# A two-layer decoder trunk on one core: the last group of the first layer's down product done with seven products, folded into the next layer by quarters

## The chip, the cores and the metric

The kernel runs on 1 core of a Trainium2 chip. The metric is the device time of one execution in microseconds (us). The engines are PE (TensorE matmul, with PEld its weight loads), DVE (VectorE), ACT (ScalarE), POOL (GpSimd) and SP (SyncE, which issues DMAs here). TensorE's granted clock is at its upper level, 2.4 GHz, through the whole execution of the kernel before (mean 0.998 of it).

## The reference, cut to what matters

```python
def reference(x, ...):                                # x: 512 tokens x 1024, float32
    for layer in range(2):
        h = rms_norm(x, g_mix[layer])
        x = x + mixer(h, ...)                         # layer 0: dilated + windowed attention; layer 1: forgetting attention
        h = rms_norm(x, g_mlp[layer])
        x = x + squared_relu_mlp(h, w_up[layer], w_down[layer])
    return x

def squared_relu_mlp(h, w_up, w_down):                # 1024 -> 4096 -> 1024
    u = jnp.einsum("bsd,df->bsf", h, w_up)
    return jnp.einsum("bsf,fd->bsd", jnp.square(jax.nn.relu(u)), w_down)
```

## The kernel before, in words

Everything is float32. A float32 product is done as three matmuls of a rounded type: each operand is split into a high part (`whi`, `hn[:, 0]`, a cast) and a low part (`wlo`, `hn[:, 1]`, operand minus high part), and hi·hi, lo·hi and hi·lo are added up in PSUM. So each weight tile passes ACT (or POOL), which casts, and DVE (or POOL), which subtracts, before PE uses it. There are 7 buffers for high and 7 for low parts.

**The MLP** (function `mlp`) is a list of `items`, run position by position; PE's work is written out in that order, and the weights of a position are prepared 6 positions ahead (`prep(n + R)`). Item `("U", u)` makes 256 of the 4096 hidden features for all 512 tokens (4 positions of 12 matmuls, 128x512). After four U items their part of the down product follows, as item `("T", g)`: a seven-product scheme for 2x2 blocks. Hidden features and tokens are halved, the output is a 2x2 grid of quarters `rest[e, t]` (512 output columns e, 256 tokens t), and seven products of sums of blocks take the place of eight. Each has 4 positions of 6 matmuls, so a T item has 28 positions and 168 matmuls, and 2 more that open the banks of `Y`. `ORDER` gives the products' order and their PSUM banks X, Y, Z; when one is done, `combine_t` adds it into a quarter on DVE, scaled by the token's 1/rms² (`r2col`). `sums_t` makes the sums of weight blocks on DVE, `t_sums` those of the hidden features.

**The end of layer 0 before.** Groups 0 to 2 are T items. The last group is done directly, as four items `("E", g, dp)`: for each pair of 128 output features, 4 positions of 12 matmuls into `dn`, output features on the partitions and tokens along the row. That is the form in which layer 1 needs its input, so `direct_end` adds `dn` to the residual (`back`), makes `hn` (hi and lo, 128x512, one tile for each of 8 chunks of features), squares it into `ssum2`, and sends it to memory (`xsp`). The quarters of groups 0 to 2 have tokens on the partitions: `fold(c)` transposes them on PE during the U items before, into `rT`, and adds them to `back`. The hidden features of the last group are scaled by 1/rms² with DVE (`part`), which needs 1/rms² along the row: a matmul with `ones` (`r2`) and reciprocals.

**The start of layer 1.** `layer_attention` projects first `v` of four heads and the forget logits (`vf_c`, 96 matmuls of 128x272 into four banks `pj0` to `pj3`, one for 128 tokens each, over the 8 chunks `hn`). After `STATS` steps of 12 matmuls it calls `stats`: `token_sums` sums squares over features (`pc`), and DVE makes 1/rms from them (`col_stats`, 13 small operations, into `rcol`). `rcol` scales the forget logits (`fz`, transposed on PE into `pz`) and `v`; then the banks `pj` are free for the next projection, of q and k (`qk_c(0)`), whose first matmul stands behind `pz` on PE. `PAT_START` and `PAT_FIRST` name the engines that cast and subtract for `vf_c`.

The last group of layer 1 is a T item already. The scheduler orders each engine's instructions; those pinned (`pin`) keep the written order.

Of the kernel before, what the change touches and what calls it, by code (L numbers as in the profile page):

```python
# [35 lines left out]
PAT_START = (('act', 'dve'), ('act', 'dve'))  # L36
WARM = 30
# [32 lines left out]
def trunk(ctx, tc, x, b_sinks, w_out_even, b_forget, w_out_odd, w_up, w_down, xt, gains, w_in_even, w_in_odd, out):  # L70
# [127 lines left out]
    def layer_attention(li, hT, w_in, w_out, stats=None):  # L198


        with ExitStack() as c2:
# [370 lines left out]
            else:  # L572
# [191 lines left out]
    def mlp(li, accs, attention_end, last):  # L764
# [7 lines left out]
        with ExitStack() as c2:  # L772
# [76 lines left out]
            def load(j):  # L849
# [52 lines left out]
            ORDER = ((11, "b11", "X"), (1, "t1", "Z"), (2, "t2", "Y"), (4, "b22", "Z"), (3, "t3", "Y"), (12, "b21", "X"),  # L902
# [41 lines left out]

            def direct(j, p, hi, lo):

                if p % 2 == 0:
                    res[j, p] = bank(("pA", "pB")[items[j][2] % 2], "dn")
                o = res[j, p - p % 2]
                for k in range(4):  # L950
                    v = store[12 + k, p % 2]
                    mm3(o, hi[:, k], lo[:, k], v[:, 0], v[:, 1], p % 2 == 0 and k == 0, bool(p % 2 and k == 3), k == 0)

            def direct_end(j, p):

                if p % 2 == 0:
                    return
                dp = items[j][2]
                c = 2 * dp + p // 2
                a = back[dp][:, p // 2]  # L960
                if c == 0:
                    res["ssum2"] = consts.tile([P, 512], F32, tag="ssum", name="ssum2")
                vec(nc.vector.tensor_add(a, res[j, p - 1], a))
                h = slot("hn")
                g = gcol[:, 8 * (li + 1) + c:8 * (li + 1) + c + 1]
                sca(nc.scalar.activation(h[:, 0], a, AF.Copy, scale=g))
                vec(nc.vector.scalar_tensor_tensor(h[:, 1], a, g, h[:, 0].bitcast(F32), op0=OP.mult, op1=OP.subtract))
                squares(c, a, res["ssum2"], sq_pool)
                hn.append(h)
                if c % 2:  # L970
                    nc.scalar.dma_start(xsp[dp], back[dp])
# [40 lines left out]
            def combine_t(j, p):  # L1012
# [4 lines left out]
                for b in range(2):  # L1017
# [12 lines left out]
                    if j == len(items) - 1 and i in (4, 3, 12, 22):  # L1030
# [11 lines left out]
            def come_back(dp):  # L1042
                a = mp.tile([P, 2, 512], F32, tag="mraw", bufs=4, name="back")
# [3 lines left out]
            def fold(c):  # L1047

                pt = bank("pB", "rT")
                for m in range(NT):  # L1050
                    pin("p", nc.tensor.transpose(pt[:, m * P:(m + 1) * P],
                                                 rest[c // 4, m // 2][:, m % 2, c % 4 * P:(c % 4 + 1) * P], ident))
                a = back[c // 2][:, c % 2]
                vec(nc.vector.tensor_add(a, pt, a))
# [14 lines left out]
            def unit_end(j):  # L1069
# [8 lines left out]
                def whole(e):  # L1078
                    s = slot("s") if u < 15 else mp.tile([P, 2, 512], F32R, tag="t24", bufs=2, name="s")
                    halves(s[:, 0], s[:, 1], v[:, e])  # L1080
                    store[u, e] = s

                def part(e):

                    sca(nc.scalar.activation(v[:, e], v[:, e], AF.Square))
                    vec(nc.vector.tensor_mul(v[:, e], v[:, e], ssum))
                    whole(e)
                    if u == 15:
                        catch_up()

                if not last and u >= 12:
                    return [lambda: part(0), lambda: part(1)]

# [12 lines left out]
                def t_part(i):  # L1106
                    if i and u % 4 == 0 and u:
# [16 lines left out]
            def plan(j):  # L1124
# [5 lines left out]
                if not last and u >= 12:  # L1130
                    offs = FIN12 if u == 12 else (0, 1)
                else:
                    offs = FIN15 if u == 15 else FIND if u % 4 == 0 and u else FIN
# [14 lines left out]
            else:  # L1148
                for dp in range(4):
                    at(LEAVE[dp], lambda dp=dp: leave(dp))  # L1150
                    at(first[16] + BACK[dp], lambda dp=dp: come_back(dp))
                for c in range(DC):
                    at(first[17] + FOLD[c], lambda c=c: fold(c))
                for n in range(8):
                    at(first[6] + n, lambda n=n: vec(nc.vector.reciprocal(ssum[:, n * 64:n * 64 + 64],
                                                                         ssum[:, n * 64:n * 64 + 64])))

            def end(n):
# [3 lines left out]
                {"U": up_end, "E": direct_end, "T": combine_t}[items[j][0]](j, p)  # L1162
                if not last and items[j] == ("U", 15):
                    if p % 2:
                        unit_end(j)[p // 2]()
                elif n + 1 == NP or pos[n + 1][0] != j:
                    plan(j)
# [15 lines left out]
            for n, (j, p) in enumerate(pos):  # L1183
# [3 lines left out]
                {"U": up, "E": direct, "T": product_t}[items[j][0]](j, p, hi, lo)  # L1187
# [58 lines left out]
```

## Time and profile before

| | before |
|---|---|
| time, median of 3 (lowest to highest) | 1157.34 us (1156.99 to 1157.52) |
| profiled execution: its own time | 1157.34 us |
| profiled execution: span of its instructions | 1155.2 us |
| PE busy, share of the span | 1140.4 us, 99% |
| DVE busy | 862.1 us, 75% |
| ACT busy | 649.2 us, 56% |
| POOL busy | 197.5 us, 17% |
| last group of layer 0, first to last matmul `dn` | 519.85 to 563.14 us |

The span is what the profiler saw of the program's instructions; 2.1 us of the time lie around it. A matmul's duration in the rows is its way through the array; matmuls overlap, and what one costs is the distance between two starts.

### The profile page before, as it was taken

What the parts mean: (1) busy time and instruction counts of PE and PEld (TensorE: products, weight loads), DVE (VectorE), ACT (ScalarE), POOL (GpSimd) and SP (SyncE); (2) the same over time, 40 slices, a digit from 0 to 9 for tenths busy, and PEclk for the clock granted to TensorE, in tenths of its full rate; (3) what the DMA queues carried; (4) which work ended last, traced back from release to release, by engine and by line L of the source; (5) the groups of instructions that cost most, each with busy time, mean ns of one, the idle gap of its engine ahead of it and who ended that gap; (6) DMA issues with size and microseconds to landing.
All of it is one profiled execution on the core that took longest, in us unless ns stands there. A gap on an engine that the chain in (4) does not pass through costs nothing.

```text
span 1155.2 us, 16365 instructions
## 1 busy us (share of the span) xinstructions
PE 1140.4 (99%) x5758; PEld 956.8 (83%) x5758; DVE 862.1 (75%) x1791; ACT 649.2 (56%) x1344; POOL 197.5 (17%) x292
## 2 busy tenths in 40 slices
PE   9999999999999999999999999999999999999998
PEld 7987887888888888888988888888888888888887
DVE  7878999967857858755647877878848759669586
ACT  7555867656656455444326675665656455465452
POOL 0445524100000000000345545432000000000000
PEclk9999999999999999999999999999999999999999
DMA  8432114530531630723543333344420722523403
GB/s 289 132 92 74 40 54 146 200 129 37 185 107 37 219 110 4 250 72 105 154 123 108 103 106 99 106 128 128 164 74 25 231 73 70 186 73 115 150 28 110
DMA packets 91329, 133.83 MB, mean 116 GB/s; under 512 B 6112, under 2 KB 54240, under 8 KB 91248
## 3 DMA queue, kind: packets, MB, share of 16 engines
q1 hardware_dynamic: 90208, 130.63, 35.5%
q10 hardware_dynamic: 1040, 2.16, 0.5%
q8 instruction: 45, 0.74, 0.3%
q14 instruction: 36, 0.29, 0.1%
HBM read 119.63 MB, written 6.32 MB: 109 GB/s over the span
## 4 chain that ended last, share of the span: by engine, by line
PE 86%; DVE 6%; DMA 2%; ACT 2%; issue 2%; POOL 1%; SPq 0%; DVEq 0%; POOLq 0%; ACTq 0%
PE up L166 10%; PE up L170 10%; PE up L169 10%; PE pj L235 4%; PE pj L237 4%; PE pj L236 4%; PE Y L999 3%; PE Y L998 3%; PE Y L996 3%; PE O L406 3%; PE PT L386 2%; PE Z L999 2%; PE X L998 2%; PE Z L998 2%; PE X L999 2%; PE X L996 2%
## 5 line engine op out<-in xcount | busy, mean ns | idle before, releaser
L166 PE MATMUL up<-xin,whi 128*128 128x512 f32 x512 | 200.8, 392 | 0.0
L794 ACT CAST whi<-wraw 128x512 fp32r<-128x512 f32 x228 | 139.3, 620 | 107.5 <-PE up L170 47.8
L170 PE MATMUL up<-xin,whi 128*128 128x512 f32 x512 | 199.4, 389 | 0.0
L169 PE MATMUL up<-xin,wlo 128*128 128x512 f32 x512 | 199.2, 389 | 0.0
L795 DVE TENSOR_TENSOR wlo<-wraw,whi 128x512 fp32r<-128x512 f32 x228 | 150.6, 686 | 61.2 <-ACT whi L794 60.6
L154 POOL TENSOR_SCALAR whi<-wraw 128x512 fp32r<-128x512 f32 x88 | 58.2, 663 | 462.3 <-PE pj L237 419.8
L170 PEld LDWEIGHTS up<-xin,whi 128*128 128x128 f32 x512 | 96.1, 188 | 20.1
L169 PEld LDWEIGHTS up<-xin,wlo 128*128 128x128 f32 x512 | 96.2, 188 | 19.8 <-issue 0.2
L166 PEld LDWEIGHTS up<-xin,whi 128*128 128x128 f32 x512 | 96.1, 188 | 19.8 <-issue 0.2
L794 ACT CAST whi<-mraw 128x512 fp32r<-128x512 f32 x112 | 68.0, 620 | 53.1 <-DVE mraw L894 22.5
L366 ACT ACTIVATE P<-P,negm 128x128 f32<-128x128 f32 (+5 forms) x128 | 69.4, 543 | 41.9 <-DVE negm L363 39.4
L943 ACT ACTIVATE u<-up 128x512 f32<-128x512 f32 x64 | 38.3, 599 | 91.8 <-PE up L170 91.8
L235 PE MATMUL pj<-whi,hn 128*128 128x512 f32 (+2 forms) x256 | 88.7, 346 | 0.0
L237 PE MATMUL pj<-whi,hn 128*128 128x512 f32 (+2 forms) x256 | 86.9, 339 | 0.0
L236 PE MATMUL pj<-wlo,hn 128*128 128x512 f32 (+2 forms) x256 | 86.8, 339 | 0.0
L795 DVE TENSOR_TENSOR wlo<-mraw,whi 128x512 fp32r<-128x512 f32 x112 | 74.5, 683 | 6.5 <-ACT whi L794 6.4
L815 DVE TENSOR_TENSOR t<-u 128x256 f32<-128x256 f32 x56 | 23.2, 423 | 68.1 <-ACT u L1076 66.2
L157 POOL TENSOR_TENSOR wlo<-wraw,whi 128x512 fp32r<-128x512 f32 x48 | 64.3, 1341 | 21.2 <-ACT whi L152 18.7
L996 PE MATMUL Y<-whi,t 128*128 128x512 f32 x168 | 65.4, 389 | 0.0
L998 PE MATMUL Y<-wlo,t 128*128 128x512 f32 x168 | 65.4, 389 | 0.0
L999 PE MATMUL Y<-whi,t 128*128 128x512 f32 x168 | 65.4, 389 | 0.0
L374 POOL TENSOR_SCALAR P<-P,rden 128x256 f32<-128x256 f32 (+2 forms) x96 | 48.5, 508 | 83.2 <-DVE rden L369 77.7
(213 smaller groups left out, 2788.4 us busy)
## 6 DMA issues: line engine op xcount, KB each, us to landing
wraw<-in_w_up SPq DMA_DIRECT2D x64, 512.0 KB, 4.5
wraw<-in_w_down SPq DMA_DIRECT2D x50, 512.0 KB, 4.1
mraw<-in_w_down SPq DMA_DIRECT2D x28, 512.0 KB, 4.8
wraw<-in_w_in_odd SPq DMA_DIRECT2D x22, 512.0 KB, 3.6
wraw<-in_w_in_even SPq DMA_DIRECT2D x17, 512.0 KB, 4.9
K<-K SPq DMA_DIRECT2D x26, 256.0 KB, 2.9
bias<-csp SPq DMA_DIRECT2D x16, 256.0 KB, 3.3
wraw<-in_w_out_odd SPq DMA_DIRECT2D x8, 512.0 KB, 3.6
```

Of the source, the lines that this page charges most:

```text
L166: m = nc.tensor.matmul(o, wh, xh, start=start, stop=False, skip_group_check=more)
L169: nc.tensor.matmul(o, wl, xh, start=False, stop=False, skip_group_check=more)
L170: nc.tensor.matmul(o, wh, xl, start=False, stop=stop, skip_group_check=more)
L235: nc.tensor.matmul(o, xh, hi[:, :n], start=k == 0, stop=False)
L236: nc.tensor.matmul(o, xh, lo[:, :n], start=False, stop=False)
L237: nc.tensor.matmul(o, xl, hi[:, :n], start=False, stop=k == DC - 1)
L366: nc.scalar.activation(p[:, :ne], p[:, :ne], AF.Exp, scale=-1.0, bias=negm[:, i:i + 1], accum_out=den[:, i:i + 1])
L794: sca(nc.scalar.copy(dst_h, src))
L795: late.append(lambda: vec(nc.vector.tensor_sub(dst_l, src, dst_h.bitcast(F32))))
L996: m = nc.tensor.matmul(o, sh, hi, start=new and k == 0, stop=False, skip_group_check=not new)
L998: nc.tensor.matmul(o, sh, lo, start=False, stop=False, skip_group_check=not new)
L999: nc.tensor.matmul(o, sl, hi, start=False, stop=k == 3, skip_group_check=not new)
```

## The change

The last group of layer 0 becomes a T item like the others. So the E items, `direct`, `direct_end`, the matmul `r2`, its reciprocals and `part` go. All quarters are now complete only in the last group, so `fold` moves there: for each quarter (e, t), when its last product is combined, two half-folds follow, each of 4 transposes, an addition of 128x512, and then, for two chunks of features and 256 tokens, the cast into `hn`, the subtraction, and the squares. `ORDER` puts b21 (X) ahead of t3 (Y) and b22 (Z) in all groups, of both layers, so the quarters become complete in the order (0,0), (1,1), (0,1), (1,0), after positions 15, 19, 23 and 27 of the group. The sums of squares of two halves of features stay apart, so `token_sums` has 8 matmuls in place of 4. `STATS` goes from 3 to 4 and `vf_c`'s low parts move from DVE to POOL.

```diff
+PAT_FIRST = (('act', 'pool'),)
-BACK = (0, 0, 1, 1)
-FOLD = (0, 0, 1, 1, 2, 2, 3, 3)
-STATS = 3
+BACK = (2, 2, 7, 7)
+FOLD = {(0, 0): 17, (1, 1): 21, (0, 1): 25, (1, 0): 28}
+STATS = 4
...
-                    return project([(512, 768), (3072, 3088)], use, PAT_START)
+                    return project([(512, 768), (3072, 3088)], use, PAT_FIRST)
...
-                if last:
-                    return
-                pr = bank("pB", "r2")
-                tc.keep_in_program_order(nc.tensor.matmul(pr, ones, ssum, start=True, stop=True))
...
-                if g < 3 or last:
-                    items.append(("T", g))
-                else:
-                    items += [("E", g, dp) for dp in range(4)]
+                items.append(("T", g))
...
-            LOADS = {-2: 11, -1: 21, 0: 22, 6: 12, 16: 220}
+            LOADS = {-2: 11, -1: 21, 0: 22, 2: 12, 16: 220}
...
-            ORDER = ((11, "b11", "X"), (1, "t1", "Z"), (2, "t2", "Y"), (4, "b22", "Z"), (3, "t3", "Y"), (12, "b21", "X"),
+            ORDER = ((11, "b11", "X"), (1, "t1", "Z"), (2, "t2", "Y"), (12, "b21", "X"), (3, "t3", "Y"), (4, "b22", "Z"),
                      (22, "t4", "Y"))
...
+            def fold(e, t, half):
+                dp = 2 * e + half
...
+                pt = bank("pB", "rT")
+                for cc in range(2):
+                    for b in range(2):
+                        pin("p", nc.tensor.transpose(pt[:, cc * 256 + b * P:cc * 256 + (b + 1) * P],
+                                                     rest[e, t][:, b, (2 * half + cc) * P:(2 * half + cc + 1) * P], ident))
+                ts = slice(t * 256, t * 256 + 256)
+                a = back[dp][:, :, ts]
+                vec(nc.vector.tensor_add(a, pt.rearrange("p (c t) -> p c t", c=2), a))
+                for cc in range(2):
...
+                    sca(nc.scalar.activation(h[:, 0, ts], a[:, cc], AF.Copy, scale=g))
+                    vec(nc.vector.scalar_tensor_tensor(h[:, 1, ts], a[:, cc], g, h[:, 0, ts].bitcast(F32),
+                                                       op0=OP.mult, op1=OP.subtract))
+                ss = res["ss"][:, :, ts]
...
+                    sca(nc.scalar.activation(sq, a, AF.Square))
+                    if (e, t) == (1, 0):
+                        vec(nc.vector.tensor_add(ss, ss, sq))
+                    else:
+                        pool(nc.gpsimd.tensor_add(ss, ss, sq))
...
+                for (e, t), n in FOLD.items():
+                    for half in range(2):
+                        at(first[-1] + n + half, lambda e=e, t=t, half=half: fold(e, t, half))
...
-            return hn, lambda: col_stats(token_sums(res["ssum2"]))
+            return hn, lambda: col_stats(token_sums([res["ss"][:, k] for k in range(2)]))
```

**DVE, in the last group of layer 0, behind the product b21 (X).** `rest_3304` is quarter (0,0) and `rest_3307` quarter (1,1); `wlo` are low parts of the group's own weights; line numbers here are those of the changed file. After the change the instructions stand so:

```order
L990 SCALAR_TENSOR_TENSOR rest_3304<-X_5419,r2col_2798,rest_3304 128x512 [waits PE_49]
L990 SCALAR_TENSOR_TENSOR rest_3304<-X_5420,r2col_2798,rest_3304 128x512 [waits PE_49]
L797 TENSOR_TENSOR wlo_5629<-mraw_5233,whi_5628 128x512 [waits Activation_49]
L797 TENSOR_TENSOR wlo_5641<-mraw_5235,whi_5640 128x512 [waits Activation_49]
L1026 TENSOR_TENSOR back_5470<-rT_5656,back_5470 128x2x256 [waits DMAHW4_49,PE_49]
L1031 SCALAR_TENSOR_TENSOR hn_5653<-back_5470,gcol_81,hn_5653 128x256 [waits Activation_49]
L1031 SCALAR_TENSOR_TENSOR hn_5654<-back_5470,gcol_81,hn_5654 128x256 [waits Activation_49]
L797 TENSOR_TENSOR wlo_5651<-mraw_5235,whi_5650 128x512
L1026 TENSOR_TENSOR back_5472<-rT_5679,back_5472 128x2x256 [waits DMAHW5_49,PE_49]
L1031 SCALAR_TENSOR_TENSOR hn_5677<-back_5472,gcol_81,hn_5677 128x256 [waits Activation_49]
L1031 SCALAR_TENSOR_TENSOR hn_5678<-back_5472,gcol_81,hn_5678 128x256 [waits Activation_49]
L797 TENSOR_TENSOR wlo_5675<-wraw_5539,whi_5674 128x512 [waits DMAHW7_49]
```

Behind these stand the two combines of quarter (1,1). Before, nothing but weights and combines stood between two products of a T item on DVE; the fold is new there, and its subtractions wait for ACT.

**PE, in the same group, at position 22.** `rT_5726` is the first half-fold of quarter (1,1), `pj0` the first matmul of layer 1's `vf_c`, which the scheduler has put between two positions of Z. The rows are those of the change:

```order
L960 MATMUL Z_5488<-whi_5628,b2_5281 128x512
L1022 MATMUL rT_5726<-ident_72,rest_3307 128x128 [waits DVE_49]
L235 MATMUL pj0_5857<-whi_5864,hn_5653 128x272 [waits Activation_49]
L1022 MATMUL rT_5726<-ident_72,rest_3307 128x128 [waits DVE_49]
L1022 MATMUL rT_5726<-ident_72,rest_3307 128x128 x2
L957 MATMUL Z_5487<-whi_5640,b2_5374 128x512
```

PE takes its instructions in this order, so it stands still at the first of them whose wait is not over. `whi_5864` is the first weight of `vf_c`; ACT casts it behind the last weight of the group.

**PE, at the sums of squares and behind `vf_c`.** Before, first to last:

```order
L621 MATMUL pc_5838<-ones_79,ssum2_5510 128x1 [waits DVE_49]
L621 MATMUL pc_5838<-ones_79,ssum2_5510 128x1 x3
L235 MATMUL pj0_5776<-whi_5822,hn_5635 128x272 [waits Activation_49]
...
L237 MATMUL pj3_5779<-whi_5914,hn_5761 128x272
L749 MATMUL pz_5947<-ident_72,fz_5942 16x128 [waits DVE_49] x3
```

and after the change:

```order
L622 MATMUL pc_5931<-ones_79,ss_5655 128x1 [waits DVE_49,PE_49]
L622 MATMUL pc_5931<-ones_79,ss_5655 128x1 x7
L237 MATMUL pj2_5859<-whi_5964,hn_5725 128x272
...
L237 MATMUL pj3_5860<-whi_5999,hn_5745 128x272
L751 MATMUL pz_6032<-ident_72,fz_6027 16x128 [waits DVE_49] x4
L235 MATMUL pj0_6057<-whi_6063,hn_5653 128x512 [waits DVE_49,PE_49]
```

Between `pc` and `pz` stood 60 of `vf_c`'s 96 matmuls; now 28 stand there.

## Rows read from the trace of the kernel before

**Rows 1.** The page's first line, its busy times, and the chain that ended last, by engine.

```profile
span 1155.2 us, 16365 instructions
PE 1140.4 (99%) x5758; PEld 956.8 (83%) x5758; DVE 862.1 (75%) x1791; ACT 649.2 (56%) x1344; POOL 197.5 (17%) x292
...
PE 86%; DVE 6%; DMA 2%; ACT 2%; issue 2%; POOL 1%; SPq 0%; DVEq 0%; POOLq 0%; ACTq 0%
```

**Rows 2.** Busy time by stage: PE, PEld, DVE, ACT, POOL (with instructions), granted clock, DMA share, GB/s. The E items lie in the first row, the start of layer 1 in the second.

```profile
520.00:570.00 50.00, 50.00 (x247) 42.52 (x246) 27.82 (x49) 20.66 (x37) 2.73 (x4) 1.00 0.41 129
570.00:600.00 30.00, 30.00 (x159) 25.87 (x158) 15.06 (x34) 9.74 (x16) 17.54 (x20) 1.00 0.42 124
```

**Rows 3.** PE's waits, summed over the span: line, who was waited for, total us, times, longest. All rows left out are of the attention and its projections too.

```profile
PE warm L632 <- DVE ones L96: 2.0, 1, 2.0
...
PE pj L235 <- DVE v L162: 0.7, 1, 0.7
```

**Rows 4.** PE in order of time at the E items' start and end: start, duration, instruction.

```profile
519.85 0.39 PE L166 MATMUL dn<-s,whi 128*128 128x512 f32 x1
...
563.14 0.39 PE L170 MATMUL dn<-s,whi 128*128 128x512 f32 x1
563.37 0.28 PE L235 MATMUL pj<-whi,hn 128*128 128x272 f32 x1
```

**Rows 5.** PE in order of time: first and last matmul of the last T item of layer 1.

```profile
1112.73 0.39 PE L996 MATMUL X<-whi,b 128*128 128x512 f32 x1
...
1151.03 0.39 PE L999 MATMUL Y<-whi,t 128*128 128x512 f32 x1
```

**Rows 6.** PE in order of time at the sums of squares in layer 0: `pc` (4 matmuls, 8 records) and `r2` (in the rows `r`).

```profile
254.70 0.95 PE L621 MATMUL pc<-ones,ssum 128*128 128x1 f32 x8
255.50 1.10 PE L826 MATMUL r<-ssum,ones 128*128 128x512 f32 x2
...
256.68 0.39 PE L169 MATMUL up<-xin,wlo 128*128 128x512 f32 x1
```

**Rows 7.** PE in order of time at two of the folds before (8 transposes) and the matmuls behind them.

```profile
497.21 1.03 PE L1051 MATMUL rT<-ident,rest 128*128 128x128 f32 x8
498.00 0.47 PE L166 MATMUL up<-xin,whi 128*128 128x512 f32 x1
498.32 0.40 PE L169 MATMUL up<-xin,wlo 128*128 128x512 f32 x1
```

**Rows 8.** DVE in order of time in the last T item of layer 1, around the end of its fourth product (Z); in brackets the idle time before a row, none here.

```profile
1130.61 1.22 DVE L894 TENSOR_TENSOR mraw<-wraw,mraw 128x1024 f32<-128x1024 f32 x1
1131.75 0.68 DVE L795 TENSOR_TENSOR wlo<-mraw,whi 128x512 fp32r<-128x512 f32 x1
1132.35 1.40 DVE L1029 SCALAR_TENSOR_TENSOR rest<-Y,r2col,rest 128x512 f32<-128x512 f32 x2
1133.67 1.88 DVE L795 TENSOR_TENSOR wlo<-mraw,whi 128x512 fp32r<-128x512 f32 x3
1135.47 0.68 DVE L795 TENSOR_TENSOR wlo<-wraw,whi 128x512 fp32r<-128x512 f32 x1
1136.07 1.40 DVE L1029 SCALAR_TENSOR_TENSOR rest<-Z,r2col,rest 128x512 f32<-128x512 f32 x2
```

**Rows 9.** PE in order of time: the first matmul behind that fourth product.

```profile
1134.94 0.39 PE L996 MATMUL Y<-whi,t 128*128 128x512 f32 x1
```

**Rows 10.** ACT in order of time behind the last E item and at the scaling of `v`.

```profile
564.30 0.72 ACT L966 ACTIVATE hn<-back,gcol 128x512 fp32r<-128x512 f32 x1 [0.31 <-DVE back L963]
...
564.93 0.62 ACT L614 ACTIVATE sqx<-back 128x512 f32<-128x512 f32 x1
...
574.94 0.84 ACT L161 ACTIVATE v<-pj,rcol 128x256 fp32r<-128x256 f32 x2 [9.09 <-DVE fz L745]
```

**Rows 11.** DVE in order of time from the sums of squares (`msv`) to the first two low parts of `v`.

```profile
568.86 0.16 DVE L141 TENSOR_SCALAR msv<-pc 128x4 f32<-128x4 f32 x1 [2.10 <-PE pc L621]
...
569.60 0.69 DVE L157 TENSOR_TENSOR wlo<-wraw,whi 128x512 fp32r<-128x512 f32 x1
...
570.40 0.48 DVE L759 MEMSET one<- 16x512 f32 x1
...
571.39 1.15 DVE L135 TENSOR_TENSOR rsq<-rsq 128x4 f32<-128x4 f32 x1
572.57 0.54 DVE L136 SCALAR_TENSOR_TENSOR rsq<-rsq 128x4 f32<-128x4 f32 x1
...
573.54 0.62 DVE L136 SCALAR_TENSOR_TENSOR rcol<-rsq 128x4 f32<-128x4 f32 x1
...
575.45 0.48 DVE L162 SCALAR_TENSOR_TENSOR v<-pj,rcol,v 128x256 fp32r<-128x256 f32 x1 [0.23 <-ACT v L161]
```

**Rows 12.** POOL in order of time in the same stretch.

```profile
571.23 1.29 POOL L157 TENSOR_TENSOR wlo<-wraw,whi 128x512 fp32r<-128x512 f32 x1
...
573.53 0.62 POOL L154 TENSOR_SCALAR whi<-wraw 128x512 fp32r<-128x512 f32 x1 [0.43 <-PE pj L237]
```

**Rows 13.** PE in order of time: the first matmul behind `pc` in layer 1, the last of `vf_c`, and the first of the next projection.

```profile
568.69 0.37 PE L235 MATMUL pj<-whi,hn 128*128 128x272 f32 x1
...
576.16 0.29 PE L237 MATMUL pj<-whi,hn 128*128 128x272 f32 x1
...
576.53 0.48 PE L235 MATMUL pj<-whi,hn 128*128 128x512 f32 x1
```

More of the change, by code (lines that the diff above doesn't have):

```diff
@@ L615, in squares, with token_sums @@
             (nc.gpsimd if c < on_pool else nc.vector).tensor_add(ssum, ssum, sq)
-    def token_sums(ssum, pin=False):
+    def token_sums(parts_, pin=False):
         pc = bank("pB", "pc")
         for t in range(NT):
-            m = nc.tensor.matmul(pc[:, t:t + 1], ssum[:, t * P:(t + 1) * P], ones[:, :1], start=True, stop=True)
-            if pin:
-                tc.keep_in_program_order(m)
+            for k, a in enumerate(parts_):
+                m = nc.tensor.matmul(pc[:, t:t + 1], a[:, t * P:(t + 1) * P], ones[:, :1], start=k == 0,
+                                     stop=k == len(parts_) - 1)
+                if pin:
+                    tc.keep_in_program_order(m)
         return pc[:, :NT]
@@ L943, in up_end @@
                     sca(nc.scalar.activation(res[j][:, p // 2], res[j, p - 1], AF.Relu))
[L945 to L971, printed above, removed]
             def product_t(j, p, hi, lo):
@@ L1029, in combine_t @@
                     vec(nc.vector.scalar_tensor_tensor(a, o, r2col[:, m:m + 1], a, op0=OP.mult, op1=OP.add))
-                    if j == len(items) - 1 and i in (4, 3, 12, 22):
+                    if last and j == len(items) - 1 and i in (4, 3, 12, 22):
                         nc.sync.dma_start(out[0, m * P:(m + 1) * P, e * 512:e * 512 + 512], a)
@@ L1042, in come_back @@
             def come_back(dp):
-                a = mp.tile([P, 2, 512], F32, tag="mraw", bufs=4, name="back")
+                tag, bufs = (("u", 2), ("u", 2), ("t", 1), ("back", 1))[dp]
+                a = mp.tile([P, 2, 512], F32, tag=tag, bufs=bufs, name="back")
                 nc.sync.dma_start(a, xmid[dp])
                 back.append(a)
-            def fold(c):
-                pt = bank("pB", "rT")
[L1050 to L1054, printed above, removed]
+            summed = set()
@@ L1076, in square @@
                         sca(nc.scalar.activation(v[:, e], v[:, e], AF.Square))
[L1078 to L1092, printed above, removed]
                 def tsum():
@@ L1106, in t_part @@
                 def t_part(i):
-                    if i and u % 4 == 0 and u:
+                    if i and (u % 4 == 0 and u or u == 15 and not last):
                         s = mp.tile([P, 2, 512], F32R, tag="t24", bufs=2, name="t24")
@@ L1129, in plan @@
                 n0 = first[j + 1]
[L1130 to L1133, printed above, removed]
+                offs = FIN15 if u == 15 else FIND if u % 4 == 0 and u else FIN
                 for i, f in enumerate(unit_end(j)):
@@ L1150, in mlp @@
                     at(LEAVE[dp], lambda dp=dp: leave(dp))
[L1151 to L1156, printed above, removed]
+                    at(first[-1] + BACK[dp], lambda dp=dp: come_back(dp))
+                for (e, t), n in FOLD.items():
+                    for half in range(2):
+                        at(first[-1] + n + half, lambda e=e, t=t, half=half: fold(e, t, half))
             def end(n):
@@ L1161, in end @@
                 j, p = pos[n]
[L1162 to L1166, printed above, removed]
+                {"U": up_end, "T": combine_t}[items[j][0]](j, p)
+                if n + 1 == NP or pos[n + 1][0] != j:
                     plan(j)
```

27 lines of the change are left out of this document (17 added, 10 removed).

## The prediction

> **What bounds the kernel now.** I read the busy times first: PE is busy for 1140.4 of 1155.2 us, and 86% of the chain that ended last is PE [rows 1]. So the end is set by how much PE has to do and by where it stands still. The stages show that it doesn't stand still where the change is made: from 520 to 570 us and from 570 to 600 us PE is busy throughout, at full granted clock, while DVE is busy for 27.8 of 50 us and POOL hardly at all [rows 2]. PE's waits name the start and the attention alone, none of an MLP matmul [rows 3]. In this stage a matmul taken from PE is therefore worth its whole cost, and a new wait of PE costs its whole length. The change does both, so both have to be counted.
>
> **The change: PE's work.** The E items are 192 matmuls, from 519.85 to 563.37 us, the start of the next one [rows 4]: 43.52 us, or 0.2267 us each. The T item has 170: 38.54 us. That a T item runs without gaps, directly behind U items, is seen in layer 1: from 1112.73 to 1151.03 + 0.23 us it took 38.53 us [rows 5]. Gain: 4.98 us. The matmul `r2` goes: from 255.50 us to the second `up` at 256.68, less the 0.23 of the first, 0.95 us [rows 6]. `token_sums` has four matmuls more, at 255.50 - 254.70 = 0.80 us for four [rows 6]: 0.80 lost. There are 32 transposes as before, but in 8 bursts, not 4; a burst costs the matmul behind it 498.32 - 498.00 - 0.23 = 0.09 us [rows 7], so 0.4 lost. PE's work shrinks by 4.98 + 0.95 - 0.80 - 0.4 = 4.7 us.
>
> The scaling of the hidden features by 1/rms² on DVE and the reciprocals go too; they are counted at nothing, since PE hid them and waited for none of them [rows 3]. The weights b21 come four positions earlier in all eight T items, behind the same SP queue; 6 positions of 1.36 us cover that. If they came late, a product would wait at the start of each group; I count nothing.
>
> **Waits in the group.** The fold ran beside U items, when DVE had room. Now it stands between the weights of the group on DVE. How full DVE is there, layer 1's T item shows: no idle time in rows 8, and the combine of the fourth product starts at 1136.07, 1.1 us after PE had gone on to the fifth at 1134.94 [rows 8, 9]. In the new order two sums of weight blocks, 1.14 us each by the distance of the starts [rows 8], stand right before that combine, not after the second product. Call this lag L: at least 1.1, at most 1.1 + 2.3 = 3.4 us; I take 2.0, a little under the middle, because DVE gets the time back earlier.
>
> From the start of the combines of quarter (0,0) DVE does, in the order shown: two combines, 1133.67 - 1132.35 = 1.32 us; two low parts at 0.60 (1.80 for three) and an addition of 0.60, so 3.1 us [rows 8]. Then it waits for ACT's cast: half of a 0.72 us instruction, 0.42 [rows 10], and the two ways there and back, some 0.67 together; two subtractions of 256 columns, 0.78 (an estimate: half the combine's 0.66, and 0.05 for the start); a low part, 0.60; the second half-fold's addition, wait and subtractions, 0.60 + 0.67 + 0.78; a low part, 0.60; and one combine of quarter (1,1), 0.66 and its way. Sum: 8.6 us. PE in the same time has 36 matmuls, 8.2 us, and two bursts of transposes at 0.5, together 9.2, before it wants that combine. It waits for L + 8.6 - 9.2 = L - 0.6 us.
>
> The `pj0` matmul behind it wants `whi_5864`, and ACT reaches that cast only behind its own folds: casts into `hn`, squares at 0.62 and the group's last casts, L + 9.6 us by the same count, while PE is past the transpose at L + 8.7. That is 0.9 us more, L + 0.3 together: 2.3 us, with bounds of 1.4 and 3.7. What is behind PE's head there is the group itself, so all of it is lost. For quarter (1,0) the same count from the transposes of (0,1) gives DVE 0.60 + 0.67 + 0.78 twice, and 0.76, so 4.9 us, against 18 matmuls and a burst, 4.6 us; with the ways in between 0.5 is lost, and about as much for (0,1): 1.0 together, with bounds of 0 (PE's free `vf_c` matmuls fill it) and 2.
>
> **Waits behind `vf_c`.** Before, the sums of squares end at 568.69 and `rcol` is there at 573.54 + 0.62 = 574.16; the first bank of `pj` is read out at 575.45 + 0.48 = 575.93 [rows 11], 7.2 us after `pc`. The 60 matmuls behind `pc` cover that: they last until 576.16 + 0.13 [rows 13], 7.6 us, or 0.13 each. Now 28 are left, 3.5 us, and the `pz` transposes, some 0.4. The chain itself keeps its length, and the matmul that waits at its end heads PE's queue: 7.2 - 3.9 = 3.3 us lost. Part of the 7.2 is not the chain's own. Three of its small operations took 1.15, 0.54 and 0.62 us, where `msv` took 0.16 [rows 11]; the first and the last end at 572.54 and 574.16, where POOL instructions end at 572.52 and 574.15 [rows 12]. Without that the chain has 7.2 - 1.8 = 5.4 us, and 1.5 is lost. Between 1.5 and 3.3 I take 2.2: as much of POOL's weight work falls beside the chain as before, but `wlo` of `vf_c` is off DVE.
>
> On these rows the Trainium skill has a rule, in "SBUF — State Buffer", section "Who interferes with whom": a DVE instruction with two SBUF inputs and a GpSimd instruction that reads SBUF exclude each other, and whoever comes first holds the port for its whole instruction. The ends just shown agree with it. By that rule moving `wlo` to POOL lengthens POOL's hold in this stretch, and the term would be the upper one, 3.3; by the row alone it is anything down to 1.5.
>
> **The sum.** -4.7 + 2.3 + 1.0 + 2.2 = +0.8 us on the profiled execution, whose own time, 1157.34 us, is also the median: 1158.1 us. The stalls at their lower bounds give -4.7 + 1.4 + 0 + 1.5 = -1.8, at their upper -4.7 + 3.7 + 2 + 3.3 = +4.3. They won't all fall to one side.
>
> **The rivals.** *Faster: the waits are hidden.* For it speaks that DVE and ACT have spare time over the stage [rows 2], so L could be near nothing, if DVE catches up before the fourth product ends. Then L - 0.6 is no wait, the wait for `whi_5864` shrinks to 0.3, the last two quarters cost 0.3, the chain 1.5: -4.7 + 2.1 = -2.6, 1154.7 us. It decides itself where the combine of (0,0) starts: under 0.5 us after PE goes on. Against it stands the 1.1 us of today, with no idle time ahead of it [rows 8, 9].
>
> *Slower: POOL holds up DVE.* POOL, idle there before, gets 8 subtractions of 272 columns (1.29 x 272 / 512, an estimate of 0.7 us each) and four additions of 1.3, most of them beside the folds of the last two quarters, whose 8 subtractions on DVE read `back` and `hn`, both in SBUF. If each waits for half a POOL instruction, some 0.4, that is 3 us more on DVE; half of it reaches PE (1.5), `pc` comes later by 0.5, and the chain costs 3.3: -4.7 + 2.3 + 1.0 + 1.5 + 0.5 + 3.3 = +3.9, 1161.2 us. The rule of the Trainium skill quoted above would have it so. It decides itself in whether the DVE subtractions of the folds (L1031) exceed 0.5 us by more than 0.2 in the mean. Against it: POOL's additions start on ACT's squares, behind the subtractions of the same half.
>
> *The T item doesn't run gapless,* because its last hidden features come from the U item just ahead. Layer 1's does [rows 5] with the same offsets; I give it 2 in 100.
>
> **Chances.** The forecast 0.52; waits hidden 0.18; POOL holds up DVE 0.28; gaps at the group's start 0.02. A change of 0.2%, 2.3 us, is about what a measurement can tell from none: faster means under 1155.0, slower over 1159.6. The forecast's own range, 1156 to 1160, lies nearly all in between. So: faster 0.18, same 0.53, slower 0.29. The range that leaves out 2 in 10 goes from 1155.0 to 1160.9.
>
> **What will show it.** In the changed profile the T item in layer 0 takes 38.5 us and the waits put into it; PE has waits for DVE at `rT` (L1022), over 1 us in all, most of it at the first half of quarter (1,1); one of about 1 us for ACT's `whi` at the first `pj`; and one of about 2 us behind `vf_c`, at `pz` and at the first matmul of `qk_c(0)`. The chain from `pc` to `rcol` has 4 to 5.5 us. The other T items still take 38.5 us. If the waits at L1022 sum to under 0.5 us the first count is wrong, and L is its step; if the wait behind `vf_c` is under 1 us, the cover is longer than 28 matmuls or the chain shorter. I would be wrong altogether if the changed weights' order opened a gap in the other seven T items: each 0.3 us would be 2 us in all.

## The result, and the profile after

The changed kernel takes 1163.62 us (median of 5 runs, 1163.05 to 1164.49) where the kernel before, run beside it, takes 1157.52 (1156.99 to 1159.54): a ratio of 1.005, 95% interval 1.0035 to 1.0065. It is 6.1 us slower; 1158.1 was forecast, and the range ended at 1160.9. The execution profiled has an own time of 1164.49 us. Line numbers below are those of the changed kernel: `pz` is L751, `fz` L747.

The page's first line and its busy times, which answer to [rows 1], and the two stages of [rows 2], in the same columns:

```profile
span 1162.7 us, 16424 instructions
PE 1138.6 (98%) x5742; PEld 953.1 (82%) x5742; DVE 880.7 (76%) x1817; ACT 661.1 (57%) x1374; POOL 210.2 (18%) x304
```

```profile
520.00:570.00 50.00, 48.17 (x254) 40.33 (x252) 43.22 (x71) 27.54 (x56) 12.87 (x12) 1.00 0.41 128
570.00:600.00 30.00, 24.68 (x120) 20.47 (x121) 15.98 (x32) 4.55 (x8) 15.54 (x19) 0.89 0.47 141
```

PE has less to do than before (1138.6 against 1140.4 us) and the span is longer, so the time is in waits. The group's stage loses 1.8 us of 50; the next one, 5.3 of 30, and its granted clock is no longer 1.00. DVE's share of the first stage has gone from 27.8 to 43.2 us. PE's waits, summed (line, who was waited for, total, times, longest), which answer to [rows 3]:

```profile
PE pz L751 <- DVE fz L747: 4.7, 1, 4.7
...
PE rT L1022 <- DVE rest L990: 1.4, 4, 0.5
...
PE pc L622 <- DVE ss L1041: 0.7, 1, 0.7
...
PE pj L235 <- ACT whi L152: 0.3, 1, 0.3
```

One wait of 4.7 us is more than all the others of this change together. To see what each stage costs, I use five marks that every kernel here has, so that the start of the execution (which differs by up to 2.5 us between profiles) falls out: the first `pc`, the first matmul of the last group, the end of `vf_c`, the first matmul of `qk_c(0)`, and the first read-out of its banks. Before, they are at 254.70 [rows 6], 519.85 [rows 4], 576.16 + 0.13 and 576.53 [rows 13], and 594.66. The last mark before, and all five after, from the rows of PE and ACT in order of time:

```profile
594.66 0.59 ACT L251 COPY qk<-pj 128x512 f32<-128x512 f32 x1 [14.30 <-PE pj L237]
```

```profile
255.47 0.72 PE L622 MATMUL pc<-ones,ssum 128*128 128x1 f32 x6
...
516.13 0.39 PE L957 MATMUL X<-whi,b 128*128 128x512 f32 x1
...
575.78 0.29 PE L237 MATMUL pj<-whi,hn 128*128 128x272 f32 x1
580.73 1.22 PE L751 MATMUL pz<-ident,fz 128*16 128x128 f32 x4 [4.67 <-DVE fz L747]
582.05 0.77 PE L235 MATMUL pj<-whi,hn 128*128 128x512 f32 x1
582.62 0.63 PE L236 MATMUL pj<-wlo,hn 128*128 128x512 f32 x1
...
601.59 0.59 ACT L251 COPY qk<-pj 128x512 f32<-128x512 f32 x1 [16.26 <-PE pj L237]
```

| us | to the last group | group and `vf_c` | behind `vf_c` | `qk_c(0)` | together |
|---|---|---|---|---|---|
| before | 265.15 | 56.44 | 0.24 | 18.13 | 339.96 |
| after | 260.66 | 59.78 | 6.14 | 19.54 | 346.12 |
| difference | -4.49 | +3.34 | +5.90 | +1.41 | +6.16 |

The +6.16 is about the 6.1 us of the medians. The two profiled spans differ by 7.5 us, 0.8 of it ahead of the first mark and 0.6 behind the last; of the seven other T items six take 38.5 us as before and one 38.9. The first column is the removed `r2` and the folds, which stood ahead of the group before.

The +5.90 is the chain from `pc` to `rcol`. DVE in order of time, to be held against [rows 11]:

```profile
572.48 0.16 DVE L141 TENSOR_SCALAR msv<-pc 128x4 f32<-128x4 f32 x1 [2.10 <-PE pc L622]
...
572.95 0.47 DVE L132 TENSOR_SCALAR rsq<-rsqb 128x4 int32<-128x4 int32 x1
573.45 0.16 DVE L134 SCALAR_TENSOR_TENSOR rsq<-msv,rsq 128x4 f32<-128x4 f32 x1
573.65 1.29 DVE L135 TENSOR_TENSOR rsq<-rsq 128x4 f32<-128x4 f32 x1
574.98 0.54 DVE L136 SCALAR_TENSOR_TENSOR rsq<-rsq 128x4 f32<-128x4 f32 x1
575.55 0.55 DVE L134 SCALAR_TENSOR_TENSOR rsq<-msv,rsq 128x4 f32<-128x4 f32 x1
576.14 0.55 DVE L135 TENSOR_TENSOR rsq<-rsq 128x4 f32<-128x4 f32 x1
576.72 0.55 DVE L136 SCALAR_TENSOR_TENSOR rsq<-rsq 128x4 f32<-128x4 f32 x1
577.31 1.20 DVE L134 SCALAR_TENSOR_TENSOR rsq<-msv,rsq 128x4 f32<-128x4 f32 x1
578.54 1.19 DVE L135 TENSOR_TENSOR rsq<-rsq 128x4 f32<-128x4 f32 x1
579.76 0.16 DVE L136 SCALAR_TENSOR_TENSOR rcol<-rsq 128x4 f32<-128x4 f32 x1
```

POOL in the same stretch, against [rows 12]:

```profile
572.19 1.20 POOL L154 TENSOR_SCALAR whi<-wraw 128x512 fp32r<-128x512 f32 x2
573.34 0.33 POOL L211 MEMSET PT<- 128x256 f32 x1
573.64 1.28 POOL L157 TENSOR_TENSOR wlo<-wraw,whi 128x512 fp32r<-128x512 f32 x1
574.89 2.37 POOL L154 TENSOR_SCALAR whi<-wraw 128x512 fp32r<-128x512 f32 x4
577.23 2.48 POOL L157 TENSOR_TENSOR wlo<-wraw,whi 128x512 fp32r<-128x512 f32 x2
```

Seven of the thirteen operations on 128x4 elements took 0.54 to 1.29 us. Each ends where a POOL instruction ends: 573.65 + 1.29 = 574.94 against POOL's 574.92; the next four at 575.52, 576.10, 576.69 and 577.27, against the four casts of 0.59 each from 574.89 (575.48, 576.08, 576.67, 577.26); the next at 578.51, and 579.73, against the two low parts (578.47 and 579.71). An eighth, L132, took 0.47 and ends at 573.42, against POOL's 573.39. The one beside the MEMSET, which reads nothing, took 0.16. From `msv` to the end of `rcol` it is 7.4 us, where it was 5.3.

The +1.41 is the clock. Busy time and granted clock (third column from the end) in slices of 2 us:

```profile
576.00:578.00 2.00, 0.07 (x1) 0.00 (x0) 1.90 (x4) 0.00 (x0) 2.00 (x4) 1.00 0.00 0
578.00:580.00 2.00, 0.00 (x0) 0.00 (x0) 1.93 (x4) 0.00 (x0) 1.71 (x2) 0.62 0.00 0
580.00:582.00 2.00, 1.19 (x4) 0.36 (x4) 1.96 (x8) 1.29 (x4) 0.00 (x0) 0.50 0.18 28
582.00:584.00 2.00, 1.95 (x5) 1.59 (x6) 1.68 (x4) 1.95 (x4) 0.00 (x0) 0.50 0.69 239
584.00:586.00 2.00, 2.00 (x8) 1.57 (x7) 0.64 (x2) 1.32 (x2) 0.00 (x0) 0.67 0.53 132
```

PE stands still, the granted clock goes from 1.00 to 0.50 (the 1.2 GHz level), and the first matmuls of `qk_c(0)` follow each other at 0.43 us, the later ones at 0.23.

### The profile page after: what moved, and what is told of

It reads as the page before. It is cut to its first block, busy times and chain, and to the rows that moved or that the text cites. A ratio compares the mean times of both kernels' runs of the same rounds, so it can differ in the third digit from the quotient of the medians.

```text
span 1162.7 us, 16424 instructions
## 1 busy us (share of the span) xinstructions
PE 1138.6 (98%) x5742; PEld 953.1 (82%) x5742; DVE 880.7 (76%) x1817; ACT 661.1 (57%) x1374; POOL 210.2 (18%) x304
## 4 chain that ended last, share of the span: by engine, by line
PE 83%; DVE 8%; DMA 3%; ACT 2%; issue 2%; POOL 1%; SPq 0%; ACTq 0%; DVEq 0%; POOLq 0%
PE up L166 10%; PE up L170 10%; PE up L169 10%; PE pj L235 4%; PE pj L237 4%; PE pj L236 4%; PE Y L957 4%; PE Y L960 4%; PE Y L959 4%; PE O L406 3%; PE X L957 2%; PE X L959 2%; PE X L960 2%; PE Z L959 2%; PE Z L957 2%; PE Z L960 2%
## 5 line engine op out<-in xcount | busy, mean ns | idle before, releaser
L797 DVE TENSOR_TENSOR wlo<-wraw,whi 128x512 fp32r<-128x512 f32 x224 | 148.2, 687 | 64.6 <-ACT whi L796 64.2
L796 ACT CAST whi<-mraw 128x512 fp32r<-128x512 f32 x128 | 77.5, 619 | 62.8 <-PE X L960 18.4
L797 DVE TENSOR_TENSOR wlo<-mraw,whi 128x512 fp32r<-128x512 f32 x128 | 85.3, 684 | 9.6 <-ACT whi L796 9.5
L817 DVE TENSOR_TENSOR t<-u 128x256 f32<-128x256 f32 x64 | 26.4, 424 | 75.0 <-ACT u L1067 72.9
L157 POOL TENSOR_TENSOR wlo<-wraw,whi 128x512 fp32r<-128x512 f32 (+1 forms) x56 | 71.1, 1276 | 25.8 <-ACT whi L152 23.5
L957 PE MATMUL Y<-whi,t 128*128 128x512 f32 x192 | 75.1, 391 | 0.0
L960 PE MATMUL Y<-whi,t 128*128 128x512 f32 x192 | 74.7, 389 | 0.0
L959 PE MATMUL Y<-wlo,t 128*128 128x512 f32 x192 | 74.7, 389 | 0.0
L1043 POOL TENSOR_TENSOR ss<-ss,sq 128x512 f32<-128x512 f32 x4 | 5.5, 1376 | 334.1 <-DVE hn L1031 329.7
```

The source lines that it names most:

```text
L157: in_order((nc.gpsimd if lo == "pool" else nc.vector).tensor_sub(dst_l, src, dst_h.bitcast(F32)))
L796: sca(nc.scalar.copy(dst_h, src))
L797: late.append(lambda: vec(nc.vector.tensor_sub(dst_l, src, dst_h.bitcast(F32))))
L957: m = nc.tensor.matmul(o, sh, hi, start=new and k == 0, stop=False, skip_group_check=not new)
L959: nc.tensor.matmul(o, sh, lo, start=False, stop=False, skip_group_check=not new)
L960: nc.tensor.matmul(o, sl, hi, start=False, stop=k == 3, skip_group_check=not new)
```

## The experiments

Three theories stood against each other. P: POOL's weight work beside the chain holds its operations, which makes the wait at `pz`. C: the chain has its length anyway, and 28 matmuls are too short a cover. G: the time goes in the group, at the folds. The table gives the same five-mark differences to the kernel before, from the rows of each kernel's profiled execution, and the chain from `msv` to the end of `rcol` (5.3 us before).

| kernel | median us | to the group | group, `vf_c` | behind | `qk_c(0)` | together | chain |
|---|---|---|---|---|---|---|---|
| changed | 1163.62 | -4.49 | +3.34 | +5.90 | +1.41 | +6.16 | 7.4 |
| e1_psum | 1159.86 | -4.45 | +3.31 | +2.90 | +1.22 | +2.98 | 4.7 |
| e2_qk_cast | 1158.09 | -4.49 | +2.90 | +0.34 | +1.68 | +0.43 | 2.4 |
| e3_lo_dve | 1164.82 | -4.49 | +10.49 | +0.73 | +0.47 | +7.20 | 2.8 |
| e4_fill | 1162.54 | -4.49 | +4.84 | +4.59 | -0.13 | +4.81 | 4.8 |
| f2_mix | 1157.37 | -4.49 | +2.89 | +0.65 | +0.83 | -0.12 | 2.7 |
| f1_fold18 | 1158.72 | -4.49 | +4.56 | 0.00 | +1.71 | +1.78 | 2.4 |
| f3_mix18 | 1157.99 | -4.49 | +3.05 | +0.65 | +0.79 | 0.00 | 2.7 |
| b1_psum | 1157.83 | -0.01 | 0.00 | 0.00 | -0.02 | -0.03 | 5.0 |
| b2_lo_pool | 1158.58 | 0.00 | +0.01 | +0.96 | +0.19 | +1.16 | 5.5 |
| b3_stats6 | 1160.86 | 0.00 | +0.02 | +2.56 | -0.02 | +2.56 | 4.2 |

The kernel before had 1157.91 beside e1, e2, e4 and b1, 1157.52 beside e3, b2, b3 and f1, and 1157.46 beside f2 and f3. The profiled executions of e1 and f1 took 1.1 and 0.8 us more than their medians, so their rows here come out higher than the medians do.

**e2: POOL off the chain.** The weights of `qk_c(0)` go to ACT and DVE, DVE's low parts held behind the chain in program order:

```diff
-        if cnt["start"]:
+        if cnt["start"] or cnt.get("q") and m.ins.engine == mybir.EngineType.DVE:
...
-                    return project([(g * 768, g * 768 + 512)], qk_use(g, 8))
+                    return project([(g * 768, g * 768 + 512)], qk_use(g, 8), PAT_ATT if g else PAT_MLP)
...
```

(`cnt["q"]` is true during `stats()` and `qk_c(0)`; the lines that set it are left out. They move `pc` to L626 and `fz` to L751.)

> The changed kernel, but the weights of the projection behind vf_c (qk_c(0)) are cast on ACT and their low parts made on DVE, behind the chain; POOL then has nothing beside the chain but the last low parts of vf_c. Theory P: the chain falls to 2.6 to 3.5 us, the wait at pz to at most 1 us, and the time to 1157.5 to 1159 us, with the operations of the chain untouched. Rival C: the chain stays at 7 us or more, 1163.6 us, or more for the work that DVE is given.

Measured 1158.09 us, 1.0004 of before (0.9995 to 1.0013). The chain of e2, whose operations are the same as the changed kernel's, first, one in the middle, and last:

```profile
571.30 0.16 DVE L141 TENSOR_SCALAR msv<-pc 128x4 f32<-128x4 f32 x1 [2.10 <-PE pc L626]
...
572.77 0.16 DVE L135 TENSOR_TENSOR rsq<-rsq 128x4 f32<-128x4 f32 x1
...
573.56 0.16 DVE L136 SCALAR_TENSOR_TENSOR rcol<-rsq 128x4 f32<-128x4 f32 x1
```

All thirteen take 0.16 or 0.17 and start 0.20 apart (one pair 0.08). The cover is as short as in the changed kernel, yet the stage behind `vf_c` falls from +5.90 to +0.34: P, and not C by itself. Nothing at the folds was touched, so G has at most the +2.90 that remains. The +1.68 of `qk_c(0)` is not the clock here (it stays at 1.00): PE waits for the read-out of `v`, 0.8 us of it in one piece, and ACT makes one of the `v` behind a cast that this edit gave it.

**e1: the operands in PSUM.** POOL keeps its work; the sums and one temporary of the chain move to columns of the bank `pc`:

```diff
-        v = small.tile([P, NT], F32, tag="msv", name="msv")
+        v, t1, y, b = [cnt["pc"][:, 8 * i:8 * i + NT] for i in (1, 2)] + [small.tile([P, NT], F32, tag=a, name="rsq") for a in ("rsq0", "rsqb")]
...
-        rsqrt_small(rcol.unsqueeze(2), v.unsqueeze(2))
+        rsqrt_small(rcol.unsqueeze(2), v.unsqueeze(2), [None, None] + [a.unsqueeze(2) for a in (y, t1, b)])
...
-        pc = bank("pB", "pc")
+        pc = cnt["pc"] = bank("pB", "pc")
```

> The changed kernel (1163.6 us), but the scaled sums and one temporary of the rsqrt chain (L132 to L136) lie in PSUM, in columns of the bank pc, so that none of the chain's operations reads two operands from SBUF. Theory P (POOL's weight work beside the chain holds each of its operations until a POOL instruction ends): the chain from msv to rcol takes 2.6 to 3.2 us (13 operations at the 0.20 that the undisturbed ones have from start to start) instead of 7.4; PE's wait for fz at pz falls from 4.7 to at most 0.8 us, the granted clock stays at 1.00, and the time is 1157.5 to 1158.5 us. Rival C (the chain has its length anyway, and 28 matmuls are simply too short a cover): the chain stays at 7 us or more and the time at 1163.6. Rival G (the time goes in the group itself, at the folds): at most 1 us is gained.

Measured 1159.86 us (1.0016, 1.0008 to 1.0025): most of the loss goes, not all, and time, chain and wait miss what I expected. PE waits 1.9 us at `pz` and 0.4 for `v`, and behind that the granted clock falls to 0.54. DVE of e1 in order of time, and POOL beside it:

```profile
572.60 0.71 DVE L132 TENSOR_SCALAR rsq<-rsq 128x4 int32<-128x4 int32 x1
573.35 0.17 DVE L134 SCALAR_TENSOR_TENSOR pc<-pc,rsq 128x4 f32<-128x4 f32 x1
573.55 0.17 DVE L135 TENSOR_TENSOR pc<-pc,rsq 128x4 f32<-128x4 f32 x1
...
575.72 1.00 DVE L157 TENSOR_TENSOR wlo<-wraw,whi 128x512 fp32r<-128x512 f32 x1
576.65 0.15 DVE L136 SCALAR_TENSOR_TENSOR rcol<-pc,rsq 128x4 f32<-128x4 f32 x1
```

```profile
572.98 0.31 POOL L211 MEMSET PT<- 128x256 f32 x1
573.25 1.28 POOL L157 TENSOR_TENSOR wlo<-wraw,whi 128x512 fp32r<-128x512 f32 x1
574.51 2.70 POOL L154 TENSOR_SCALAR whi<-wraw 128x512 fp32r<-128x512 f32 x3
```

Every operation of the chain with an operand in PSUM took 0.14 to 0.17 while POOL worked without a pause. That is what the Trainium skill says in "SBUF — State Buffer", section "Who interferes with whom": a DVE instruction with at most one SBUF input, outside the modes in which DVE uses two ports, doesn't contend with GpSimd; one with two does, with a GpSimd instruction that reads SBUF. The rows of those operations agree. L132 is another case: it has one input, in SBUF, and was held all the same, in the changed kernel to the end of a POOL cast, here to the end of the MEMSET (573.31 against 573.29). Whether it ran in one of those modes no trace shows. What kept the chain at 4.7 us, against the 2.6 to 3.2 expected, is L132 and what was scheduled between the last steps: two low parts of weights, one of them at 1.00 us instead of 0.69, and a memset of 0.48.

**b1: the same edit in the kernel before.**

> The kernel before (1157.5 us) with the same move of the chain's operands to PSUM. Theory P: its chain falls from 5.3 to 2.6 to 3.2 us (four of its operations were held); since 60 matmuls cover it, only the 0.7 us wait for v can go: 1156.8 to 1157.5 us. Rival C: the chain keeps 5.3 us, and the time 1157.5.

Measured 1157.83 us (1.0002, 0.9994 to 1.0011), no change. The chain fell only to 5.0: its own operations took 0.14 to 0.17, but DVE's order has weight work ahead of `rcol` that waits for POOL's cast. Under 60 matmuls that costs nothing.

**e3: the low parts of `vf_c` back on DVE,** one part of the change undone:

```diff
-                    return project([(512, 768), (3072, 3088)], use, PAT_FIRST)
+                    return project([(512, 768), (3072, 3088)], use, PAT_START)
```

> The changed kernel with the low parts of vf_c's weights back on DVE, as before the change (PAT_START); the rest of the change stays. pc then stands before the last 22 matmuls of vf_c, not 28. Theory P says that this part of the change pushed POOL's weight work for the next projection into the stretch of the chain: without it POOL starts that work earlier, the chain falls from 7.4 to 4.5 to 6 us, and the wait at pz from 4.7 to 2 to 3.5; DVE has 8 low parts of 272 columns more between the folds, which may cost 0.5 to 2 us in the group: 1161 to 1164 us. If the chain stays at 7 us or more, moving the low parts to POOL was not what lengthened it, and the time is 1164 us or more, by the six matmuls of cover that are lost.

Measured 1164.82 us (1.0065, 1.0052 to 1.0078). The chain was free (2.8 us, below what I expected), so the edit does decide when POOL starts on the next weights; but the loss came back ahead of it, and the time is above the 1161 to 1164 I expected. PE, DVE and POOL of e3 in order of time:

```profile
573.99 3.31 PE L622 MATMUL pc<-ones,ss 128*128 128x1 f32 x16 [4.84 <-DVE ss L1041]
```

```profile
568.94 0.82 DVE L1031 SCALAR_TENSOR_TENSOR hn<-back,gcol,hn 128x256 fp32r<-128x256 f32 x1
569.68 1.74 DVE L157 TENSOR_TENSOR wlo<-wraw,whi 128x512 fp32r<-128x512 f32 x1
571.35 0.82 DVE L1031 SCALAR_TENSOR_TENSOR hn<-back,gcol,hn 128x256 fp32r<-128x256 f32 x1
572.10 1.74 DVE L1041 TENSOR_TENSOR ss<-ss,sq 128x512 f32<-128x512 f32 x1
```

```profile
569.46 1.42 POOL L157 TENSOR_TENSOR wlo<-wraw,whi 128x512 fp32r<-128x512 f32 x1
570.85 1.05 POOL L154 TENSOR_SCALAR whi<-wraw 128x512 fp32r<-128x512 f32 x1
```

The last quarter's folds now have POOL beside them. A subtraction of 256 columns takes 0.82 us and an addition 1.74, where `ss` took 0.69 in the changed kernel; `pc` is 4.8 us late, and PE comes back from that wait at half clock. DVE also has more to do in this stretch, the low parts of `vf_c` and one of 512 columns: some 2.5 us from 563 to 574 by the spacing of undisturbed ones (0.38 and 0.60). The excess of the held rows over undisturbed ones is some 5 us there. Both are estimates from the rows; no run parts them. By them the larger share is again POOL's work beside DVE work that PE waits for.

**b2: that part of the change alone,** in the kernel before (`PAT_START` to `(('act', 'pool'),)` in the same line).

> The kernel before (1157.9 us) with the low parts of vf_c's weights on POOL (the change's PAT_FIRST alone). Theory P: POOL's work for the next projection moves later and the chain gets longer than 5.3 us, up to 7; 60 matmuls (7.5 us) still cover it, so the time moves by at most 1 us: 1157.5 to 1159 us. If the chain stays at 5.3 us or falls, POOL's weight work is not pushed into it by this edit alone.

Measured 1158.58 us (1.0008, 0.9998 to 1.0017), as expected in time; the chain stayed at 5.5, so this edit alone does not push POOL's weight work into it. By itself the move of the low parts to POOL costs about 1 us.

**b3: the cover alone.** `STATS = 6` in the kernel before leaves 24 matmuls behind `pc`.

> The kernel before (1157.9 us) with pc placed later: 24 of vf_c's matmuls are left behind it instead of 60, nothing else is changed. It measures what the short cover costs by itself. If the chain keeps the 5.3 us it has before, fz comes 5.8 us behind pc's sums, 24 matmuls cover 3.0, and PE waits some 2.5 to 3 us at pz: 1160.5 to 1161 us with the clock at 1.00, up to 1162.5 if it falls behind the wait as in the changed kernel. If POOL's work were spread out so that it doesn't meet the chain here, the chain would be 2.5 to 3.5 us, and the time 1158 to 1159.

Measured 1160.86 us (1.0028, 1.0018 to 1.0039), PE waiting behind `vf_c` for 2.56 us more, at a granted clock of 1.00. So a short cover costs some 2.6 us where the chain has 4.2 us, about the size of my own term (2.2). C is a part of the loss: it takes both, a short cover and a held chain. With a chain of 2.4 us a cover of 28 matmuls costs 0.3 (e2), and with a cover of 60 a chain of 5.5 costs 1.0 (b2).

**e4: PE kept busy.** 80 idle matmuls ahead of the `pz` transposes:

```diff
         pz = bank("pB", "pz")
+        for _ in range(80):
+            nc.tensor.matmul(pz[:, :P], identb, identb, start=True, stop=True)
```

> The changed kernel with 80 idle matmuls of 128 columns (bf16 identity) on PE right before the pz transposes, where PE stands still for 4.7 us. They change no wait. Theory: the granted clock of 0.5 behind the standstill comes from the standstill; then the clock stays at 1.00, the first eight matmuls of qk_c(0) follow each other at 0.23 instead of 0.43 us, and 1.6 to 2 us are gained: 1161.6 to 1162.0 us. Rival: the clock falls for another reason (DVE, POOL or the DMAs), or the fill delays pz: 1163.6 us or more.

Measured 1162.54 us (1161.58 to 1164.36), 1.1 us less than the changed kernel, less than expected. Slices of e4, columns as above:

```profile
572.00:574.00 2.00, 2.00 (x11) 2.00 (x11) 1.93 (x3) 0.00 (x0) 2.00 (x3) 0.50 0.03 12
...
580.00:582.00 2.00, 2.00 (x14) 1.66 (x11) 0.00 (x0) 1.36 (x3) 0.81 (x1) 1.00 0.89 238
582.00:584.00 2.00, 2.00 (x10) 1.67 (x9) 0.18 (x1) 1.77 (x2) 0.60 (x1) 1.00 0.75 266
```

Behind the fill the clock stays at 1.00 and `qk_c(0)` loses nothing (-0.13 instead of +1.41), so the fall there did come from the standstill. What ate the rest: in this execution the clock had already fallen earlier, at 572 to 574 us, behind the wait for `pc` and its one-column matmuls, and `vf_c` took 1.5 us longer. The chain was 4.8 us long here with the same instructions (POOL, which waited 1.2 us for PE at 574.1, had two casts beside it and not four), so the fill, not `fz`, set the time of `pz`.

**f1, f2, f3: towards a better version.** f1 is e2 with the folds of quarter (0,0) one position later; f2 is e2 with the last four of the eight weight tiles cast on POOL, which falls mostly behind the chain; f3 is both. The edits of f1 and f2 on e2:

```diff
-FOLD = {(0, 0): 17, (1, 1): 21, (0, 1): 25, (1, 0): 28}
+FOLD = {(0, 0): 18, (1, 1): 21, (0, 1): 25, (1, 0): 28}
...
-                    return project([(g * 768, g * 768 + 512)], qk_use(g, 8), PAT_ATT if g else PAT_MLP)
+                    return project([(g * 768, g * 768 + 512)], qk_use(g, 8), PAT_ATT if g else (("act","dve"),)*1+(("pool","dve"),)*4+(("act","dve"),)*3)
```

> The version with qk_c(0)'s weights on ACT and DVE (1158.1 us) and the first quarter's folds one position later (FOLD 18 in place of 17), so that DVE gives the weight blocks of the fifth product their turn first. If PE's waits at the folds (1.4 us at rT and 0.3 at whi) come from DVE's folds of (0,0) standing ahead of the combine of (1,1), they fall by 0.3 to 0.8 us: 1157.3 to 1157.8 us. If they come from DVE's load as a whole, they only move to the next quarter: 1158.1 us or more.

> The version with qk_c(0)'s weights off POOL (1158.1 us), but the last four of its eight weight tiles are cast on POOL again (their low parts stay on DVE, behind the chain). These four come after rcol, and ACT no longer has a cast between the scalings of v, which cost PE 0.8 us at the first matmuls of qk_c(0). Theory P: only what runs beside the chain does harm, so the chain stays at 2.3 to 3.5 us, and the wait for v falls to 0.3: 1157.3 to 1157.8 us. Rival: POOL's casts hold up the chain's end or the scaling of v on DVE all the same: 1158.5 to 1160 us.

> The same, with the folds of the first quarter one position later (FOLD 18). If the loss at the folds is DVE's order, 1156.5 to 1157.3 us; if it only moves to the next quarter, as FOLD 18 showed when it was tried before, 1157.3 to 1158.5 us.

Measured: f1 1158.72 us (1.0006, 0.9998 to 1.0015), f2 1157.37 (0.9998, 0.9989 to 1.0007), f3 1157.99 (1.0003, 0.9994 to 1.0011). In f1 PE's waits at the folds are 1.5 us in two pieces, instead of 1.4 in four: they only moved, which speaks for DVE's load and against its order. f2 is level with the kernel before; what `qk_c(0)` loses at the read-out of `v` (0.8 us) did not fall to the 0.3 I expected. No version beats the kernel before.

## Why the prediction was wrong

- **PE's work: right.** Forecast -4.7. By the marks it is -4.49 ahead of the group, and 59.78 less the waits below, against 56.44: -0.06; together -4.55.
- **Waits in the group: right in place, the sizes off both ways.** Forecast 2.3 + 1.0. The starts of PE's rows show 1.2 us more than the spacing at the first half of quarter (1,1) and at the `whi` behind it, below the bound of 1.4, and 1.4 for quarters (0,1) and (1,0): 2.6. The lag L was 1.1 us, its lower bound, and not 2.0. From the rows of PE and DVE:

```profile
538.34 0.39 PE L957 MATMUL Y<-whi,t 128*128 128x512 f32 x1
```

```profile
539.48 1.40 DVE L990 SCALAR_TENSOR_TENSOR rest<-X,r2col,rest 128x512 f32<-128x512 f32 x2
```

- **The sums being late: missed.** In the sum I had `pc` starting without a wait; it waits 0.7 us for the last addition, 0.8 with the restart. I had 0.5 of it in a rival only. In e2, where POOL has no cast beside the first `ss` of quarter (1,0), that addition takes 0.68 us instead of 1.10 and `pc` waits 0.2: some 0.4 of the 0.8 is POOL's hold too.
- **Waits behind `vf_c`: the step that failed.** Forecast 2.2, bounds 1.5 and 3.3; measured 5.9. The 28 matmuls of cover were counted well (572.30 to 575.91, 3.6 us). What failed was "the chain itself keeps its length", with "as much of POOL's weight work falls beside the chain as before". The bound of 3.3 took the 7.2 us of the kernel before as the longest, though 1.8 us of it was POOL's hold on a few operations, and nothing in the rows limits that hold to a few. In the changed kernel POOL comes late to its work for `qk_c(0)`, behind the low parts of `vf_c`, for whose last weights it waits 3.0 us on ACT, and does that work without a pause beside the chain: eight operations were held, and from `msv` to `rcol` it is 7.4 us instead of 5.3. e2 shows the same chain at 2.4. These 2.1 us are most of the 2.6 above the bound. A smaller error is the 0.4 of cover counted for the `pz` transposes: they wait for `fz` and cover nothing.
- **The clock behind the stall: not in the sum.** 1.4 us more (e4).
- **The rivals.** "POOL holds up DVE" had the mechanism and the sign, and named the wrong place: the subtractions at L1031 in the changed kernel take 0.89 to 1.47 us for two, 0.50 each in the mean of all sixteen, so by its own deciding point (0.7) it would have been ruled out. "The waits are hidden" is out: the combine of (0,0) starts 1.1 us after PE goes on, not under 0.5.

The sum with the measured terms: -4.55 + 2.6 + 0.8 + 5.9 + 1.4 = +6.15. Without POOL's work beside the chain the change is level with before (e2, f2), close to the forecast, but not by its sum: what the seven products save, 4.55 us, is used up by some 3 us of waits in the group and for the sums, where DVE is now busy 43 of 50 us, and by 2.0 (e2) or 1.5 us (f2) behind `vf_c` and at the read-out of `v`.

## What to carry to other kernels

A chain of tiny DVE operations on SBUF that PE waits for has no fixed length: the thirteen here took 2.4 us with POOL idle and 7.4 with POOL at work. A held operation lasted to the end of the POOL instruction beside it, so an upper bound is the number of operations times the POOL instruction (0.59 or 1.24 us here), and not the length in the trace of before. When a change moves work to POOL, look at what POOL then does later, and beside what. The remedies tried here, bulk work taken off POOL for that stretch (e2) or one operand of each operation in PSUM (e1), took back nearly all and half of the loss there (from 5.9 us to 0.3 and to 2.9).

## What was unexpected of the hardware

The granted clock fell to 0.50 in two kernels without a long standstill: in e4 and f1, from about 571 to 575 us, while PE was busy (2.00 of 2.00 us in the slice shown), behind a wait of 0.7 us in e4 and 0.2 in f1 and `pc`'s sixteen one-column matmul records (1.92 us). In the changed kernel, e1, e2, f2 and f3 the same `pc` left the clock at 1.00. Why it fell in some executions and not in others is open; in both it costs some 1.5 us of `vf_c`. It may be what spreads the times of one kernel: of f1's eleven runs the five with a mean granted clock of 1.00 took 1156.8 to 1158.0 us, the six below it 1158.7 to 1159.7.
